# Moving modulation steps, DFT products and small loads in one step of a hybrid GLA and Fourier backbone

## The chip, the cores and the metric

The kernel runs on one core of a Trainium2 chip. The metric is the device time of one execution in microseconds (us), median of several runs. A profiled execution gives a trace of every instruction: TensorE (PE in the profile; PEld is its weight load), VectorE (DVE), ScalarE (ACT), GpSimd (POOL), and SP, which here only issues DMAs. All times below come from that profile or from the timed runs.

## The reference

One layer of a diffusion backbone for 128 context tokens and 256 latent tokens, 2048 channels, float32. Cut to what matters here:

```python
mod = jax.nn.silu(cond) @ lw['w_ada'] + lw['b_ada']
sh1, sc1, ga1, sh2, sc2, ga2 = [m[:, None, :] for m in jnp.split(mod, N_MOD, axis=-1)]
h = rmsnorm(x, lw['norm_pre_mix']) * (1.0 + sc1) + sh1
...
proj = h @ lw['w_in']                  # q, k, v, output gate g, two low-rank factors, Fourier channels fo
o = gla(q, k, v, decays)               # bidirectional gated linear attention, 4 heads
o = norm(o) * jax.nn.silu(g)
fg = fo.astype(jnp.float32).reshape(bsz, t, FOURIER_GROUPS, FOURIER_GROUP_DIM)
f = jnp.fft.fft2(fg, axes=(1, 3), norm='ortho').real
gates = jax.nn.sigmoid(h @ lw['w_gate'] + lw['b_gate'])
g_a, g_b = jnp.split(gates, 2, axis=-1)
merged = g_a * (o @ lw['w_br_gla']) + g_b * (f @ lw['w_br_four'])
return merged @ lw['w_out'], s_f, s_b
...
x = x + ga1 * rmsnorm(m, lw['norm_post_mix'])
h = rmsnorm(x, lw['norm_pre_ffn']) * (1.0 + sc2) + sh2
ff = (jax.nn.silu(h @ lw['w_ffn_gate']) * (h @ lw['w_ffn_up'])) @ lw['w_ffn_down']
x = x + ga2 * rmsnorm(ff, lw['norm_post_ffn'])
```

The six modulation vectors come from a product of one vector per token kind (context, latent) with a matrix of 2048 x 12288. The first two (sh1, sc1) are needed at once and are made on TensorE. Of the others, ga1 is needed by the output projection and sh2, sc2 by the FFN's input; these three, with the numbers 2, 3 and 4, are the "modulation steps" of this text.

## The kernel before

Activations lie transposed, channels on the 128 partitions and the 384 tokens along a row. A product in full float32 precision is made of three passes: every operand is split into a high part (`whi`, `A_hi`) and a low part (`wlo`, `A_lo`) of a reduced type, and high by high, high by low and low by high are summed.

**Weights.** A weight tile is 128 x 1024 (half a MB). `load` (L213) has SP fetch it into one of two `raw` buffers. `split` casts it to `whi` on ScalarE (L255) and subtracts on VectorE to `wlo` (L256); four pairs of buffers hold the results. `grab` takes the oldest ready pair, then loads one tile and splits one, so the split runs up to three tiles ahead of its use. For a tile of the Fourier projection (`fold`, L222 and L223) VectorE first adds and subtracts halves; for the two tiles of a DFT group it adds and subtracts the two raw tiles (L239, L240) and then splits both results (L316).

**Order.** PE, ScalarE, VectorE and GpSimd execute in the order in which the code is written. Side work is interleaved by generators: after every half unit (24 matmuls of 384 columns) `step` advances them. `paced(gen, rate)` advances one by `rate` calls to a step on average.

**Stages that the change touches**, in order of time:

- The head (up to 146 us): the normalised input is made and v is projected. `fold_h` adds and subtracts mirrored positions of h; `keep_h` (L417) stores the two halves of the folded h to DRAM, both by SP.
- 24 gate units (`gate_unit`, L673, L674), with GLA beside the first 22, one generator call to a half unit. In each head GpSimd clears `att` (L721) and `am` (L813), which VectorE then fills by masked copies. In the first 16 gate units SP also loads `wnr` (L902): the first column of 16 weight tiles, single words, needed by VectorE once (L933) behind gate unit 21.
- The DFT stage, gate units 24 to 31. Each is followed by two tiles of the Fourier input projection (`pfo`, L1038, L1039). After every second unit a group of 256 channels is complete; VectorE ends it in `fs` (L1043). The generator `dft` then makes products over channels (`px`, L995, L996 and L1001), copies them to `xc` and `nyq` (L997, L998, L1002), and makes products over positions in its next call (`pp`, L980, L981, L985).
- The output gates ("o", eight of them, `gcol`) and the Fourier projections ("b", sixteen, `four`), in the order of `mix_order` (L172): numbers of b behind each o are 0, 0, 1, 2, 2, 2, 1, 2. `nyq_weights` (L1058 to L1069) builds weights for the Nyquist row beside the first of them. `gate_of` fetches the sigmoid gate of a coming unit. Then come the GLA projections ("a") with the remaining b.
- The output projection (`wout`, 16 units), and behind it the FFN.

**Modulation steps.** `ada_rest` is a generator. For each of 3 vectors and each of 2 halves it makes 16 calls in which SP loads half a MB of `w_ada` (L621) and VectorE multiplies it by the condition of both token kinds and adds it to `adacc` (L624, L626); one empty call; one in which PE sums over partitions (`pr`, L634); and the next one begins by turning the result (`ptm`, L643) and adding biases. How many calls fall into each stage is set by `rate`:

```python
rate[0] = 1.0     # heads, 22 gate units;  0.5 in gate units 22 and 23;  1.0 in the DFT stage
rate[0] = 0.75    # output gates; 0.0 in Fourier and GLA projections
rate[0] = 0.7     # output projection
if i == KT - 4:   # behind its unit 12: whatever is left
    for _ in ada_gen:
        pass
```

Of the kernel before, what the change touches and what calls it, by code (L numbers as in the profile page):

```python
# [11 lines left out]
F32 = mybir.dt.float32  # L12
# [9 lines left out]
P = 128  # L22
# [85 lines left out]
def tile_step(ctx: ExitStack, tc: tile.TileContext, a, o):  # L108
# [60 lines left out]

    mix_order, n_b = [], 0  # L170
    for i in range(8):
        k = (0, 0, 1, 2, 2, 2, 1, 2)[i]  # L172
        mix_order += [("o", i)] + [("b", n_b + j) for j in range(k)]
        n_b += k
    for i in range(KT):
# [173 lines left out]
    with ExitStack() as s:  # L349
# [64 lines left out]
            ACT.copy(f[:, HL : HT : HC - 1], h[:, 0:HC : HC - 1])  # L414

        def keep_h(q):
            SP.dma_start(hf_d[:, 8 * q : 8 * q + 8, :], xnt[q])  # L417

        scr = actp.tile([P, 8, T], F32, tag="B_lo", name="scr")
        pv = [psm.tile([P, 512], F32, tag="mm", name="pv") for _ in range(3)]  # L420
# [257 lines left out]
    with ExitStack() as s:  # L678
# [20 lines left out]
        def chunks(x):  # L699
            return x.rearrange("p (t c i) -> p t c i", t=3, c=2)  # L700

        def gla():
            def split2(tags, src):
                out = [pg.tile([P, src.shape[1], src.shape[2]], F32R, tag=t, name="part") for t in tags]
# [8 lines left out]
            for h in range(NH):  # L713
# [5 lines left out]
                ACT.copy(krs, kr)  # L719
                att = pg.tile([P, 3, P], F32, tag="att", name="att")  # L720
                POOL.memset(att, 0.0)  # L721
                s0 = []
                for d in range(2):
                    s0.append(pg.tile([P, 1, DV], F32, tag=f"s0{d}", name="s0"))
# [86 lines left out]
                yield  # L811
                am = pg.tile([P, 3, CH], F32, tag="am", name="am")
                POOL.memset(am, 0.0)  # L813
                DVE.copy_predicated(am, mask[:, 1:2, :].to_broadcast([P, 3, CH]), ats[1])
                for c in range(2):
                    v = att[hf(c), :, c * CH : (c + 1) * CH]
# [80 lines left out]
        for i in QK[1:]:  # L897
            proj(psm, hT, keep(qk, i), sd)
        for i in range(GF):
            if i < 16:  # L900
                src = a["w_in"][16 + i // 2, i % 2].rearrange("p (k c) -> p k c", c=P)[:, :, 0]
                SP.dma_start(wnr[:, i // 2, 8 * (i % 2) : 8 * (i % 2) + 8], src)  # L902
            gate_unit(i, sd)
        for _ in gl:
            pass
# [3 lines left out]
    with ExitStack() as s:  # L909
# [67 lines left out]
        def dft():  # L977

            def even(dst, stat):
                PE.matmul(dst, stat(0, P), cd[:, D_TA : D_TA + HT], start=True, stop=False)  # L980
                PE.matmul(dst, stat(1, HC + 1), cd[0 : HC + 1, D_TB : D_TB + HT], start=False, stop=True)  # L981

            def odd(dst, stat):
                for k, m, c0, o0, o1 in ((0, HL - 2, D_SA, HC, HT), (1, HC - 2, D_SB, 0, HC)):
                    PE.matmul(dst[:, o0:o1], stat(k, m), cd[0:m, c0 : c0 + o1 - o0], start=True, stop=True)  # L985

            for g in range(4):
                while done[0] < g + 1:
                    yield
                fe, fd = fs[g]  # L990
                xc = [pf_.tile([P, 2, 2, P], F32, tag=f"xc{m}", name="xc") for m in range(2)]
                px = pss.tile([P, 2, 129], F32, tag="side", name="px")
                cb = D_CB + 129 * g
                for t, (p0, m) in enumerate(((0, P), (P, HC + 1))):
                    PE.matmul(px[0:m, t], fe[:, p0 : p0 + m], cd[:, D_CE : D_CE + 129], start=True, stop=False)  # L995
                    PE.matmul(px[0:m, t], bn[:, p0 : p0 + m], cd[:, cb : cb + 129], start=False, stop=True)  # L996
                    ACT.copy(xc[0][0:m, t], px[0:m, t, 0:P].unsqueeze(1).to_broadcast([m, 2, P]))  # L997
                    ACT.copy(nyq[0:m, t, g : g + 65 : 32], px[0:m, t, P : P + 1].to_broadcast([m, 3]))  # L998
                px = pss.tile([P, 2, P], F32, tag="side", name="px")
                for t, (p0, m) in enumerate(((0, HL - 2), (HL - 2, HC - 2))):  # L1000
                    PE.matmul(px[0:m, t], fd[:, p0 : p0 + m], cd[:, D_CS : D_CS + P], start=True, stop=True)  # L1001
                    ACT.copy(xc[1][0:m, t], px[0:m, t].unsqueeze(1).to_broadcast([m, 2, P]))  # L1002
                yield
                off = (P - 32 * g) % P
                rot = [x.rearrange("p t r c -> p t (r c)") for x in xc]
                for m, (x, part) in enumerate(((eT, even), (dT, odd))):
                    pp = pss.tile([P, HT], F32, tag="side", name="pp")
                    part(pp, lambda k, n: rot[m][0:n, k, off : off + P])
                    split_act(x[g][:, 0:HT], x[g][:, HT:], pp)
                yield  # L1010
            pn = pss.tile([P, HT], F32, tag="side", name="pn")
            even(pn, lambda k, n: nyq[0:n, k, :])
            ACT.copy(pnr, pn)
            DVE.tensor_sub(pnr[64:96], pn[64:96], pnr[64:96].bitcast(F32))
            yield
# [8 lines left out]

        sd = side()
        rate[0] = 1.0
        for i in range(FO0, 32):
            gate_unit(i, sd)
            g, kh = divmod(i - FO0, 2)
            if kh == 0:  # L1030
                pfo = [psm.tile([P, 2 * n], F32, tag="mm", name="pfo") for n in (HT, HO)]
                fs[g] = [pf_.tile([P, n], F32, tag=f"fs{j}", name="fs") for j, n in enumerate((HT, HO))]
            for j, n in enumerate((HT, HO)):
                w, p = grab(), pfo[j]
                for k in range(8):
                    x = xo[kh][:, k, :] if j else xe[:, 8 * kh + k].rearrange("p a c -> p (a c)")
                    c = slice(k * P, (k + 1) * P)
                    PE.matmul(p, w[0][:, c], x[:, 0 : 2 * n], start=kh == k == 0, stop=False)  # L1038
                    PE.matmul(p[:, 0:n], w[1][:, c], x[:, 0:n], start=False, stop=kh == 1 and k == 7)  # L1039
                if kh:  # L1040
                    f = fs[g][j]
                    ACT.copy(f, p[:, n : 2 * n])
                    DVE.tensor_add(f, f, p[:, 0:n])  # L1043
            if kh:
                done[0] = g + 1
        sx.close()
        fold_in.clear()
        pc = s.enter_context(tc.tile_pool(name="pc", bufs=1))
# [4 lines left out]
        def nyq_weights():  # L1053

            n = D // 2
            for h in range(2):
                wr = pc.tile([P, n], F32, tag="ws", name="wr")
                POOL.memset(wr, 0.0)  # L1058
                for g in range(4):
                    src = a["w_br_four"][8 * h : 8 * h + 8, 32 * g : 32 * g + 1, (2 * g + 1) * P : (2 * g + 2) * P]  # L1060
                    SP.dma_start(
                        wr[g : g + 65 : 32, :].rearrange("p (i c) -> p i c", c=P),
                        src.rearrange("i p c -> p i c").to_broadcast([3, 8, P]),
                    )
                    if g % 2:
                        yield
                w = wn[:, n * h : n * h + n]
                ACT.copy(w, wr)
                DVE.tensor_sub(w[32:64], wr[32:64], w[32:64].bitcast(F32))  # L1069
                yield  # L1070
# [67 lines left out]
        mT, late = None, []  # L1138
        for b, i in mix_order:
            if b == "o":  # L1140
                rate[0] = 0.75
                if i == 2:
                    gate_of()
                proj(psm, hT, lambda p: gcol(p, i), sd)
                if i == 2:
                    gate_of()
                rate[0] = 0.0
                continue
# [23 lines left out]
    with ExitStack() as s:  # L1172
# [42 lines left out]
            ACT.activation(sq2, mg32(i), AF.Square)  # L1215
            return sq0, pr, sq2

        rate[0] = 0.7
        spare_h = {-4: ((pe, "hid_hi", 1), (pe, "hid_lo", 1)), -2: ((pe, "S0", 1), (pe, "S1", 1))}
        spare_w = ((adap, "adaw", 2), (adap, "adaw", 2))  # L1220
        raw2 = None
# [926 lines left out]
```

## Time and profile before

| | us |
|---|---|
| median of 3 runs | 1976.55 (1975.61 to 1977.62) |
| the profiled execution | 1978.45 |
| its span, first to last instruction | 1976.7 |
| PE busy | 1912.3 (97%) |
| VectorE busy | 1673.7 (85%) |
| ScalarE busy | 1078.3 (55%) |
| GpSimd busy | 145.4 (7%) |
| mean granted TensorE clock | 0.990 |

Rows of the profile are read as follows. A group of instructions has its line, engine, operation, the tiles written and read, its shape and count, then busy time, mean length in ns, and the idle time of the engine just before, with what ended it. A list of waits has the waiting instruction, the one that released it, the total in us, how often, and the longest. A timeline has start, length and instruction, and in brackets the idle time before it. In a row by stage the window is followed by its length and by busy us and count of each engine, the granted clock, the share of DMA time and GB/s. Matmuls overlap, and their ends are modelled, so a PE that is always busy is not one at its peak.

### The profile page before, as it was taken

Reading aid. Unit: us, or ns where it says so; the run is one execution under the profiler, and the core shown is the slowest. Engines: PE = TensorE matmul, PEld = TensorE weight load, DVE = VectorE, ACT = ScalarE, POOL = GpSimd, SP = SyncE. Lnnn points to the kernel's source line nnn. Section 1 sums busy time; section 2 is a strip of 40 time slices with the busy share of each in tenths; the row PEclk is TensorE's granted clock in tenths of the full one; section 3 lists DMA queues with packets and bytes.
Section 4 is the critical chain, followed back from the end, with each engine's and each line's share of the span. In section 5 each row is a group of like instructions: output and inputs, shape, how many; then the busy total and the mean of one; then the engine's idle time right before and its main releaser. Section 6 shows DMA issues by size and latency. Waiting matters only on the chain.

```text
span 1976.7 us, 27848 instructions
## 1 busy us (share of the span) xinstructions
PE 1912.3 (97%) x10284; PEld 1682.4 (85%) x10284; DVE 1673.7 (85%) x2136; ACT 1078.3 (55%) x1566; POOL 145.4 (7%) x172
## 2 busy tenths in 40 slices
PE   8999999999998889997999999999999999999998
PEld 5778899998998789997998888888888888888886
DVE  5676898868758897796879999999999999988885
ACT  4234455453344555443746666666676766666555
POOL 0000000000000000000400021111111111202001
PEclk9999999999999999998999999999999999999999
DMA  9988666776655687565527796979697988969653
GB/s 390 370 300 222 231 221 229 249 259 226 206 191 171 207 276 268 180 206 176 205 93 241 200 253 167 277 155 279 146 267 171 245 199 221 235 155 241 168 196 125
DMA packets 263657, 435.65 MB, mean 220 GB/s; under 512 B 62044, under 2 KB 166684, under 8 KB 258912
## 3 DMA queue, kind: packets, MB, share of 16 engines
q1 hardware_dynamic: 216576, 393.23, 59.7%
q0 software_dynamic: 18432, 33.56, 11.2%
q10 hardware_dynamic: 28512, 7.08, 2.2%
q8 instruction: 80, 1.31, 0.3%
q14 instruction: 57, 0.47, 0.1%
HBM read 369.05 MB, written 57.67 MB: 216 GB/s over the span
## 4 chain that ended last, share of the span: by engine, by line
PE 82%; DVE 9%; DMA 4%; ACT 3%; issue 2%; SPq 0%; POOL 0%; DVEq 0%; ACTq 0%; POOLq 0%
PE pgu L1664 30%; PE pmm L289 23%; PE pdn L1664 10%; PE pds L1664 7%; DVE adacc L626 3%; PE pv L447 3%; DMA raw<-in_w_in 2%; DVE wlo L256 2%; PE pgm L430 1%; PE pfo L1038 1%; PE px L465 1%; PE pmm L1378 1%; ACT whi L255 1%; DMA adaw<-in_w_ada 1%; PE bk L1664 1%
## 5 line engine op out<-in xcount | busy, mean ns | idle before, releaser
L289 PE MATMUL pmm<-A_hi,wlo 128*128 128x384 f32 x1072 | 362.9, 339 | 5.4 <-DVE wlo L256 5.3
L289 PE MATMUL pmm<-A_hi,whi 128*128 128x384 f32 x1072 | 366.1, 341 | 0.0
L289 PE MATMUL pmm<-A_lo,whi 128*128 128x384 f32 x1072 | 362.5, 338 | 0.0
L1562 ACT CAST whi<-u 128x1024 fp32r<-128x1024 f32 x200 | 210.3, 1053 | 171.2 <-PE pds L1664 39.3
L1573 DVE TENSOR_TENSOR wlo<-u,whi 128x1024 fp32r<-128x1024 f32 x200 | 244.2, 1222 | 33.5 <-ACT whi L1562 29.0
L256 DVE TENSOR_TENSOR wlo<-raw,whi 128x1024 fp32r<-128x1024 f32 x163 | 198.7, 1222 | 69.9 <-ACT whi L255 69.3
L255 ACT CAST whi<-raw 128x1024 fp32r<-128x1024 f32 x165 | 172.7, 1050 | 152.3 <-DMA raw<-in_w_gate 52.4
L1664 PE MATMUL pgu<-whi,A_hi 128*128 128x512 f32 x640 | 249.9, 390 | 0.0
L1664 PE MATMUL pgu<-whi,A_lo 128*128 128x512 f32 x640 | 249.1, 389 | 0.0
L626 DVE SCALAR_TENSOR_TENSOR adacc<-adaw,cond,adacc 128x1024 f32<-128x1024 f32 x180 | 222.8, 1280 | 2.8 <-DMA adaw<-in_w_ada 2.6
L1562 ACT CAST whi<-raw 128x1024 fp32r<-128x1024 f32 x157 | 165.0, 1052 | 92.3 <-PE pgu L1664 25.8
L289 PEld LDWEIGHTS pmm<-A_hi,wlo 128*128 128x128 f32 x1072 | 204.1, 190 | 7.6 <-DVE wlo L256 7.3
L289 PEld LDWEIGHTS pmm<-A_hi,whi 128*128 128x128 f32 x1072 | 204.6, 191 | 4.3 <-issue 2.7
L289 PEld LDWEIGHTS pmm<-A_lo,whi 128*128 128x128 f32 x1072 | 204.3, 191 | 0.2
L1573 DVE TENSOR_TENSOR wlo<-raw,whi 128x1024 fp32r<-128x1024 f32 x157 | 191.6, 1221 | 12.4 <-ACT whi L1562 12.1
L1664 PE MATMUL pgu<-wlo,A_hi 128*128 128x512 f32 x640 | 185.8, 389 | 0.0
L1664 PEld LDWEIGHTS pgu<-whi,A_hi 128*128 128x128 f32 x640 | 120.1, 188 | 25.9 <-issue 0.8
L1664 PEld LDWEIGHTS pgu<-wlo,A_hi 128*128 128x128 f32 x640 | 120.1, 188 | 25.1
L1664 PEld LDWEIGHTS pgu<-whi,A_lo 128*128 128x128 f32 x640 | 120.1, 188 | 24.8
L1664 PE MATMUL pgu<-whi,S 128*128 128x512 f32 x400 | 116.6, 389 | 0.0
L1797 POOL DMA_DIRECT2D sums_d<-spare x64 | 58.4, 948 | 624.7 <-ACT spare L1793 607.8
L1664 PE MATMUL pdn<-whi,hid_hi 128*128 128x512 f32 x264 | 102.8, 389 | 0.0
(455 smaller groups left out, 3521.2 us busy)
## 6 DMA issues: line engine op xcount, KB each, us to landing
adaw<-in_w_ada SPq DMA_DIRECT2D x96, 512.0 KB, 3.7
raw<-in_w_d SPq DMA_DIRECT2D x70, 512.0 KB, 5.8
slab<-in_w_ada SPq DMA_DIRECT2D x32, 1024.0 KB, 9.0
raw<-in_w_gate SPq DMA_DIRECT2D x64, 512.0 KB, 4.5
raw<-in_w_g SPq DMA_DIRECT2D x48, 512.0 KB, 3.7
raw<-in_w_u SPq DMA_DIRECT2D x48, 512.0 KB, 5.1
u<-in_w_u SPq DMA_DIRECT2D x40, 512.0 KB, 5.6
u<-in_w_g SPq DMA_DIRECT2D x40, 512.0 KB, 9.3
```

What stands on the lines that cost most here:

```text
L255: ACT.copy(hi, raw)
L256: sub = lambda: eng.tensor_sub(lo, raw, hi.bitcast(F32))
L289: PE.matmul(dst, w[wi][:, k * n + n0 : k * n + n0 + P], x[xi][:, k0 + k, :], start=first and k == 0 and j == 0, stop=last and k == kts - 1 ...
L430: PE.matmul(pgv[q : q + 32, :], spad[:, k, :], slab[k // (KT // 2)][:, k % (KT // 2), :], start=k < 4, stop=k >= KT - 4,)
L447: PE.matmul(pv[2 * t + g], hT[x_][:, kb, t * P : (t + 1) * P], w_[:, g * 512 : (g + 1) * 512], start=kb == 0 and j == 0, stop=kb == KT - 1 ...
L465: PE.matmul(px, w_[:, u * P : (u + 1) * P], hT[x_][:, kb, :], start=j == 0, stop=j == 2)
L626: DVE.scalar_tensor_tensor(acc[:, c, :], w, cond[:, k, c : c + 1], acc[:, c, :], op0=ALU.mult, op1=ALU.add,)
L1038: PE.matmul(p, w[0][:, c], x[:, 0 : 2 * n], start=kh == k == 0, stop=False)
L1562: ACT.copy(hi, src)
L1573: DVE.tensor_sub(lo, src, hi.bitcast(F32))
L1664: PE.matmul(dst, stat[x_][m], mov(w[w_], m), start=first and w_ == m == x_ == 0, stop=last and w_ == m == 1, skip_group_check=any(more),)
L1797: POOL.dma_start(sums_d[k], u, accum_op=ALU.add)
```

## The change

- `mix_order`: the numbers of b behind each o become 0, 1, 1, 2, 1, 2, 1, 2. The two calls of `gate_of` go from output gate 2 to output gate 1.
- The rate at the output gates is 1.0 for the first two and 0.25 for the other six (0.75 before). In the DFT stage a second pacer on the same generator adds half a call for each of the two tiles of `pfo`. In the output projection the rate is 0.77 (0.7 before).
- In `dft` all products over channels of a group are issued ahead of the copies that read them; the second group of products has its own name, `py`.
- The second half of the folded h is stored by ScalarE's queue.
- The sixteen loads of single words go from SP to GpSimd's queue, as `column(n)`: two behind the memset of `att` in heads 1 to 3, two behind the memset of `am` in each head, two more in the last.
- The buffer `wr` in `nyq_weights` has its own place; before, it shared one with the folded weight tiles.

```diff
@@ mix_order
-        k = (0, 0, 1, 2, 2, 2, 1, 2)[i]
+        k = (0, 1, 1, 2, 1, 2, 1, 2)[i]
@@ keep_h
-            SP.dma_start(hf_d[:, 8 * q : 8 * q + 8, :], xnt[q])
+            (ACT if q else SP).dma_start(hf_d[:, 8 * q : 8 * q + 8, :], xnt[q])
@@ new function
+        def column(n):
+
+            src = a["w_in"][16 + n // 2, n % 2].rearrange("p (k c) -> p k c", c=P)[:, :, 0]
+            POOL.dma_start(wnr[:, n // 2, 8 * (n % 2) : 8 * (n % 2) + 8], src)
@@ gla
                 POOL.memset(att, 0.0)
+                if h:
+                    column(4 * h - 2)
+                    column(4 * h - 1)
...
                 POOL.memset(am, 0.0)
+                column(4 * h)
+                column(4 * h + 1)
+                if h == NH - 1:
+                    column(14)
+                    column(15)
@@ gate units
-            if i < 16:
-                src = a["w_in"][16 + i // 2, i % 2].rearrange("p (k c) -> p k c", c=P)[:, :, 0]
-                SP.dma_start(wnr[:, i // 2, 8 * (i % 2) : 8 * (i % 2) + 8], src)
@@ dft
                 for t, (p0, m) in enumerate(((0, P), (P, HC + 1))):
                     PE.matmul(px[0:m, t], fe[:, p0 : p0 + m], ..., start=True, stop=False)
                     PE.matmul(px[0:m, t], bn[:, p0 : p0 + m], ..., start=False, stop=True)
+                py = pss.tile([P, 2, P], F32, tag="side", name="py")
+                for t, (p0, m) in enumerate(((0, HL - 2), (HL - 2, HC - 2))):
+                    PE.matmul(py[0:m, t], fd[:, p0 : p0 + m], cd[:, D_CS : D_CS + P], start=True, stop=True)
+                for t, m in enumerate((P, HC + 1)):
                     ACT.copy(xc[0][0:m, t], px[0:m, t, 0:P].unsqueeze(1).to_broadcast([m, 2, P]))
                     ACT.copy(nyq[0:m, t, g : g + 65 : 32], px[0:m, t, P : P + 1].to_broadcast([m, 3]))
-                px = pss.tile([P, 2, P], F32, tag="side", name="px")
-                for t, (p0, m) in enumerate(((0, HL - 2), (HL - 2, HC - 2))):
-                    PE.matmul(px[0:m, t], fd[:, p0 : p0 + m], cd[:, D_CS : D_CS + P], start=True, stop=True)
-                    ACT.copy(xc[1][0:m, t], px[0:m, t].unsqueeze(1).to_broadcast([m, 2, P]))
+                for t, m in enumerate((HL - 2, HC - 2)):
+                    ACT.copy(xc[1][0:m, t], py[0:m, t].unsqueeze(1).to_broadcast([m, 2, P]))
@@ DFT stage
         rate[0] = 1.0
+        more = paced(ada_gen, [0.5])
...
                     DVE.tensor_add(f, f, p[:, 0:n])
-            if kh:
-                done[0] = g + 1
+                    if j:
+                        done[0] = g + 1
+                step(more)
@@ nyq_weights
-                wr = pc.tile([P, n], F32, tag="ws", name="wr")
+                wr = pc.tile([P, n], F32, tag="wr", name="wr")
@@ output gates
-                rate[0] = 0.75
-                if i == 2:
+                rate[0] = 1.0 if i < 2 else 0.25
+                if i == 1:
                     gate_of()
                 proj(psm, hT, lambda p: gcol(p, i), sd)
-                if i == 2:
+                if i == 1:
                     gate_of()
@@ output projection
-        rate[0] = 0.7
+        rate[0] = 0.77
```

## The prediction

> **What bounds the kernel now.** I read the page's busy shares and slices first, then the list of what TensorE (PE) waited for, then busy time by stage.
>
> ```profile
> PE   8999999999998889997999999999999999999998
> DVE  5676898868758897796879999999999999988885
> ```
>
> PE is busy all along, with dips at both ends, in the slices from 593 to 741 us and in the one from 890 (49.4 us each). So a gain can only come out of named gaps. The list of PE's waits names them (us in total, times, longest):
>
> ```profile
> PE pf L1113 <- DVE wlo L256: 10.3, 9, 1.5
> PE pr L634 <- DVE adacc L626: 10.1, 1, 10.1
> PE pmm L289 <- DVE wlo L256: 6.0, 6, 2.5
> PE px L995 <- ACT nyq L998: 5.8, 4, 4.2
> PE at L797 <- DVE ki L774: 5.1, 2, 4.6
> ...
> PE pf L1112 <- ACT whi L255: 2.2, 1, 2.2
> PE px L1001 <- ACT xc L1002: 2.2, 4, 0.6
> ```
>
> Stage by stage (window, length, then busy us and instructions of PE, its weight loads, VectorE, ScalarE, GpSimd; granted clock): the DFT stage, the first two output gates, the other gates with the Fourier projections, the output projection up to its unit 12 (with the last GLA projections), and what follows that unit.
>
> ```profile
> 452.90:578.20 125.30, 118.31 (x722) 114.39 (x719) 97.92 (x96) 48.54 (x77) 0.95 (x1) 0.97 0.64 204
> 578.20:609.00 30.80, 29.70 (x176) 28.89 (x175) 16.38 (x19) 11.51 (x21) 0.95 (x1) 1.00 0.46 153
> 609.00:709.00 100.00, 81.51 (x465) 75.52 (x464) 87.07 (x141) 52.77 (x78) 0.00 (x0) 0.98 0.67 220
> 779.00:895.00 116.00, 116.00 (x681) 115.07 (x679) 95.77 (x117) 51.83 (x83) 0.00 (x0) 1.00 0.61 198
> 895.00:912.00 17.00, 6.27 (x31) 4.25 (x30) 10.58 (x15) 2.01 (x5) 0.00 (x0) 0.61 0.40 129
> ```
>
> From 609 to 709 VectorE is busy 87% and PE stands still for 18.5 us, which are the first, third and sixth rows of the waits (10.3 + 6.0 + 2.2). The clock drops behind a gap, too; the same columns for three short windows:
>
> ```profile
> 489.10:495.90 6.80, 6.34 (x22) 5.71 (x21) 3.99 (x4) 2.11 (x5) 0.00 (x0) 0.50 0.73 233
> 615.30:618.70 3.40, 3.40 (x13) 3.40 (x12) 2.82 (x4) 2.08 (x3) 0.00 (x0) 0.51 0.92 322
> 707.50:710.90 3.40, 3.40 (x15) 3.40 (x15) 3.12 (x9) 2.83 (x7) 0.00 (x0) 0.50 0.62 202
> ```
>
> Half clock for 3.4 us costs 1.7 us of work.
>
> **The moved modulation steps.** One step is two products and sums on VectorE, half a MB loaded by SP, and every 17th and 18th call has no product. The first row is the page's cost; the others count such instructions by stage.
>
> ```profile
> L626 DVE SCALAR_TENSOR_TENSOR adacc<-adaw,cond,adacc 128x1024 f32<-128x1024 f32 x180 | 222.8, 1280 | 2.8 <-DMA adaw<-in_w_ada 2.6
> ```
> ```profile
> 452.90:578.20 125.30, 1.45 (x18) 0.70 (x18) 36.06 (x30) 0.37 (x1) 0.97 0.64 204
> 578.20:609.00 30.80, 0.00 (x0) 0.00 (x0) 4.96 (x4) 0.00 (x0) 1.00 0.46 153
> 609.00:709.00 100.00, 0.00 (x0) 0.00 (x0) 24.75 (x20) 0.00 (x0) 0.98 0.67 220
> 895.00:912.00 17.00, 2.85 (x18) 0.69 (x18) 7.35 (x6) 0.37 (x1) 0.61 0.40 129
> ```
>
> A step is 2 x 222.8/180 = 2.48 us of VectorE. The generator makes 109 calls. Before: 58 up to unit 23, 16 in the DFT stage (74), 16 x 0.75 = 12 at the output gates (86), 26 x 0.7 = 18 in the output projection (104), and 5 drained behind its unit 12. After: 58, 16 + 16 x 0.5 = 24 (82), 4 + 12 x 0.25 = 7 (89), 26 x 0.77 = 20 (109): nothing is left to drain. As products: 8 pairs (19.8 us of VectorE) more in the DFT stage, 6 pairs (14.9 us) fewer from 578 to 709, of which 8 fewer from 609 on and 2 more before it.
>
> *End of the drain.* VectorE's timeline there:
>
> ```profile
> 897.98 4.87 DVE L626 SCALAR_TENSOR_TENSOR adacc<-adaw,cond,adacc 128x1024 f32<-128x1024 f32 x4
> 904.04 2.48 DVE L626 SCALAR_TENSOR_TENSOR adacc<-adaw,cond,adacc 128x1024 f32<-128x1024 f32 x2 [1.19 <-DMA adaw<-in_w_ada]
> ```
>
> PE reduces `adacc` only behind these. After, the last pair is due at half-unit 23 (17/0.77) and the reduction at 25, 8 us later, so PE does not wait. The window 895 to 912 holds 31 matmuls: 18 of the reduction, which take 1.45 us at full clock (the 452.9 row), and 13 of the projection at 116/681 = 0.17 us, 3.7 us in all. Gain 17 - 3.7 = **13.3 us**. Its price: 16 pairs in 23 half-units (23 x 24 x 0.17 = 94 us) are 39 us; the rest of VectorE's work in 779 to 895 is 95.8 - 36 (15 pairs) = 60 in 116, or 48 in 94. 87 of 94 us: it still fits. If ScalarE's share does not let it, 4 us are lost (a rival below). I take 13.
>
> *Fourier projections.* What PE loses from 578 to 709 is 18.5 us, 2 x 1.7 of clock, and behind each of 16 gaps the modelled tail of a matmul (it lasts 0.34 and the next follows at 0.17), 2.7: 24.6 us. Without it the stage needs 130.8 - 24.6 - 1.1 (the fourth `px`) = 105 us of PE. VectorE: 16.4 + 87.1 - 14.9 = 88.6 busy, and waits that lie in its own chain (its groups in 609 to 709, idle time last):
>
> ```profile
> L256 DVE TENSOR_TENSOR wlo<-ws,whi 128x1024 fp32r<-128x1024 f32 x11 | 13.4, 1222 | 5.8 <-ACT whi L255 5.8
> ...
> L316 DVE TENSOR_TENSOR o_lo<-gs,o_hi 128x384 fp32r<-128x384 f32 x7 | 3.9, 558 | 4.1 <-ACT o_hi L315 4.1
> ```
>
> 98.5 us: under 105, but nearly level, so place decides. By pattern: two Fourier units and a gate now take VectorE about 16 us (window rows), PE 13.5; at rate 0.25 a pair fewer, 13.5. One Fourier unit and a gate: 9.7 against 11. The new order alternates them, so PE leads from the second unit on. The weak place is the first: unit b0 moves from behind the third gate to behind the second, where VectorE has 4 pairs, b0's fold and the copy of the Nyquist weights:
>
> ```profile
> 602.26 1.21 DVE L1069 TENSOR_TENSOR wn<-wr,wn 32x1024 fp32r<-32x1024 f32 x1 [2.73 <-ACT wn L1068]
> ```
>
> b0 itself reads only the first half of `wn`, but this second copy (behind a GpSimd memset and four DMAs) holds VectorE's queue, and queued behind it stand the split for o2's second half and b1's fold. I lay that queue out with these durations: o2's second half is about 3 us late, b1 about 4, each with one window of half clock: 10 us. Bounds: 0 (the wait falls into slack) to 16 (VectorE stays level to the end). Gain 24.6 - 10, I take **14 us** (8 to 24). The own buffer for `wr` only takes a dependency off; nothing.
>
> The Trainium skill, "TensorE: Matmul & The Clock Gate", Part 1, says that the clock falls to half after an idle window of about 3.4 us. This trace shows half clock at 615.3 behind a gap of 2.5 us at most; the measurement decides. By the page those clock windows would not hang on the gaps, and the stage would give 3 us less, 1945 in all.
>
> **DFT products ahead of copies.** Matmuls into `px` row tile 1 waited for ScalarE to read row tile 0 (fourth and last row of the waits, 8.0 us), and the 4.2 us gap of the first group brought 6.8 us of half clock, 3.4: 11.4 us. ScalarE's and PE's timeline:
>
> ```profile
> 485.91 1.05 ACT L315 CAST whi<-ws 128x1024 fp32r<-128x1024 f32 x1 [5.84 <-DVE ws L239]
> 487.17 1.04 ACT L315 CAST whi<-rp 128x1024 fp32r<-128x1024 f32 x1 [0.21 <-DVE rp L240]
> 488.12 0.36 ACT L997 COPY xc<-px 128x256 f32<-128x256 f32 x1
> ```
>
> The copies are not faster; they stand behind casts that wait for VectorE's `ws` and `rp`. After, PE goes on with half a gate unit (4.1 us), and needs the copies only at `pp`. Against it come the 8 pairs. VectorE: 97.9 + 19.8 = 117.7 us against 125.3 - 10 = 115: level again. Two calls without products (71, 72) fall to the third group, so groups 3 and 4 are free; in groups 1 and 2 the added pair before `fs` (2.48, less some 1.3 that VectorE idled there) makes `px` wait 1, and the one between `fs` and `ws` makes `pp` wait 2 and 1.4. 11.4 - 4.4 = **7 us**. Bounds: 11.4 if all is covered, and -8.4 if all 19.8 are exposed; nearer the first, since VectorE has 27 idle us here and 14 more up to 609. The moved steps bring their loads along, 8 x 0.5 MB: 204 GB/s (the stage row's last column) becomes some 240, and each waits on SP for a buffer that VectorE frees, with the next weight load queued behind; that follows VectorE's pace and adds no term of its own.
>
> **Folded h and single words.** One 1.5 MB store goes to ScalarE's queue: one issue (0.4 us, as SP's second row below) where ScalarE waits for the same fold anyway: nothing. The sixteen word loads leave SP's queue:
>
> ```profile
> L902 SPq DMA_DIRECT2D wnr<-in_w_in x16: 545/678/2943, 165.5 to 186.6; - x16
> ...
> 188.13 0.38 SPq L213 DMA_DIRECT2D raw<-in_w_in  x1
> ...
> 192.71 1.05 ACT L255 CAST whi<-raw 128x1024 fp32r<-128x1024 f32 x1 [7.56 <-DMA raw<-in_w_in]
> ```
>
> The load at 188 stood behind them, and the wait of `at` (5.1) is downstream of it. But SP then waits for free buffers instead, so I expect the load under 1 us sooner. Bounds 0 and 5.1 + 1.7; **1 us**. On GpSimd each costs between the mean of its present DMAs and eight times that (1,024 words against 128 rows):
>
> ```profile
> L1797 POOL DMA_DIRECT2D sums_d<-spare x64 | 58.4, 948 | 624.7 <-ACT spare L1793 607.8 <-DMA u<-in_w_g 10.4 <-ACT whi L1562 6.5
> ...
> L797 PE MATMUL at<-qi,ki x96: 222/222/356, 197.1 to 381.3; 128*64 128x64 f32 x96
> ```
>
> 0.95 to 7.6 us, four to a head, and a head lasts about 60 us ((381.3 - 197.1)/3): 4 x 7.6 = 30, covered, with the memsets of `att` and `am` queued behind.
>
> **Sum.** 7 + 14 + 13 + 1 = 35 us. The profiled execution took 1978.45 (span 1976.7 and 1.75 around it): 1943.5. It is 1.9 above the median 1976.55, so **1941.5 us**.
>
> **Rivals.** (a) *VectorE becomes the bound of the DFT stage*: for it, 117.7 against 115; against, the idle time up to 609. Then that term is -8.4, and its delay leaves 10 of the Fourier term: 16 us, 1961. (b) *No new wait at b0 and b1, none at `pp`*: 11 + 22 + 13 + 1 = 47, 1929.5; for it, that PE holds up to three weights ready. (c) *VectorE is full in the output projection*: 4 us less, 1945.5; for it, 87 of 94 us. (d) *The waits only move*, since VectorE's total is unchanged: what is left is the end of the half clock at 489, 3 us, 1973.5; against, 40 idle us of VectorE before 609. (e) *Slower: the word loads hold GpSimd.* Place: `att` and `am` memsets behind them, with VectorE's masked copies, then weights, waiting. From 15 us a load (60/4) each head slips by 4t - 60; over four heads this eats the 35 us at t = 17. At 25 us it is 160 us, 2101. Against: even the slowest present rate by count is 7.6.
>
> The Trainium skill, "SBUF — State Buffer", SBUF: two separate sides, says that GpSimd's descriptors starve while VectorE runs a two-port operation; it gives 3,100 ns for a DMA of 620. By that ratio, 5 x 7.6 = 38 us, (e) would hold. No run here shows it: GpSimd's DMAs at 0.95 us lie beside VectorE's two-input operations, and these are also what fills the heads.
>
> **Chances.** Forecast 0.45, (a) 0.20, (b) 0.17, (c) 0.10, (d) 0.04, (e) 0.04. Range 1927 to 1962: from under (b) to over (a). About 0.2% (4 us) is what a measurement tells from no change: faster 0.92, same 0.04, slower 0.04.
>
> **What would show it.** Right: no wait of `px` on `nyq`, no `pr` wait near 900, under 12 us of `pf`/`pmm` waits from 578 to 709, the first at o2 or b1; SP without `wnr`. Wrong: waits of PE on `wlo` in the DFT stage (a), on `pmm` before 895 (c), VectorE waiting for GpSimd's memsets (e).

## The result and the profile after

The changed kernel takes **1946.05 us**, median of 4 runs (1945.23 to 1947.25), against 1976.2 (4 runs, 1975.61 to 1977.62) of the kernel before: a ratio of 0.9847, 95% interval 0.983 to 0.9864, or 30.2 us faster. The forecast was 1941.5, and the range (1927 to 1962) holds the time. The profiled execution took 1945.23 us, its span is 1943.3.

The page's busy shares and the slices of PE and VectorE, of the kernel after (a slice is 48.6 us):

```profile
PE 1901.4 (98%) x10284; PEld 1676.0 (86%) x10284; DVE 1671.0 (86%) x2136; ACT 1078.5 (55%) x1568; POOL 159.4 (8%) x188
...
PE   8998999999998999999999999999999999999997
...
DVE  5677888878997797987789999999999999988985
```

The dips that stood between 593 and 741 us and at 890 are gone but for one 8 at 583 to 632. VectorE's count of instructions is what it was; its work sits earlier.

The list of PE's waits from 459 to 760, kernel after (us in total, times, longest):

```profile
PE pf L1127 <- DVE wlo L256: 5.0, 6, 1.5
PE pf L1126 <- ACT whi L255: 2.0, 1, 2.0
PE py L1009 <- DVE fs L1056: 1.6, 1, 1.6
PE pmm L289 <- DVE wlo L256: 1.5, 1, 1.5
PE pfo L1052 <- DVE wlo L316: 0.8, 1, 0.8
PE pp L990 <- ACT xc L1011: 0.7, 2, 0.3
PE pfo L1051 <- ACT whi L315: 0.5, 1, 0.5
PE pf L1129 <- DVE edT L1026: 0.5, 1, 0.5
```

`px` waits for no `nyq` any more, and no `pr` waits for `adacc`. The windows used in the prediction no longer cut the same work, so from here on stages are bounded by named instructions of PE: the first `pfo` (DFT), the first `pt` (transposes of the first output gate), the last `pf` (end of the Fourier projections), the first `pst` (behind the output projection), the first `bk` (last block). The stage rows of before and then of after (window, length, busy us and instructions of PE, its weight loads, VectorE, ScalarE, GpSimd; granted clock, DMA share, GB/s):

```profile
461.38:589.63 128.25, 120.16 (x731) 115.68 (x731) 94.47 (x94) 48.87 (x81) 0.95 (x1) 0.97 0.67 213
589.63:764.54 174.91, 156.42 (x909) 150.20 (x908) 151.26 (x254) 90.68 (x141) 0.95 (x1) 0.98 0.68 223
764.54:935.29 170.75, 160.02 (x927) 157.08 (x927) 131.40 (x165) 73.44 (x118) 0.00 (x0) 0.96 0.60 197
...
1945.26:1976.70 31.44, 22.49 (x121) 18.28 (x119) 17.96 (x53) 16.90 (x47) 6.41 (x5) 0.95 0.35 101
```
```profile
459.42:580.34 120.92, 117.24 (x732) 112.66 (x731) 112.89 (x111) 45.63 (x80) 0.96 (x1) 1.00 0.80 249
580.34:742.82 162.48, 153.35 (x909) 149.78 (x907) 135.67 (x240) 93.94 (x143) 0.96 (x1) 0.98 0.70 227
742.82:899.79 156.97, 156.97 (x926) 155.24 (x926) 126.55 (x164) 73.68 (x118) 0.00 (x0) 1.00 0.63 209
...
1910.13:1943.30 33.17, 22.49 (x121) 18.28 (x119) 17.95 (x53) 16.90 (x47) 6.40 (x5) 0.94 0.33 95
```

The DFT stage is 7.3 us shorter although VectorE does 18.4 us more in it; the Fourier stage 12.4 shorter; in the output projection PE is busy for all of 156.97 us, 13.8 shorter. What lies ahead of them ("heads" in the table below) is 2.0 shorter. Up to the last block the gain is 35.1 us. Then the last row: the same matmuls, the same busy times on every engine, and **1.7 us longer**. Left of the span's gain: 33.4.

### The profile page after: what moved, and what is told of

The parts are those of the page before. It is cut to its first block, busy times and chain, and to the rows that moved or that the text cites. A ratio compares the mean times of both kernels' runs of the same rounds, so it can differ in the third digit from the quotient of the medians.

```text
span 1943.3 us, 27865 instructions
## 1 busy us (share of the span) xinstructions
PE 1901.4 (98%) x10284; PEld 1676.0 (86%) x10284; DVE 1671.0 (86%) x2136; ACT 1078.5 (55%) x1568; POOL 159.4 (8%) x188
## 4 chain that ended last, share of the span: by engine, by line
PE 82%; DVE 8%; DMA 4%; ACT 3%; issue 2%; SPq 0%; POOL 0%; ACTq 0%; DVEq 0%; POOLq 0%
PE pgu L1678 31%; PE pmm L289 23%; PE pdn L1678 10%; PE pds L1678 7%; PE pv L447 3%; DVE adacc L626 3%; DMA raw<-in_w_in 2%; PE pgm L430 1%; DVE wlo L256 1%; DMA slab<-in_w_ada 1%; PE px L465 1%; PE pmm L1392 1%; PE bk L1678 1%; DMA adaw<-in_w_ada 1%; ACT whi L255 1%
## 5 line engine op out<-in xcount | busy, mean ns | idle before, releaser
L1587 DVE TENSOR_TENSOR wlo<-u,whi 128x1024 fp32r<-128x1024 f32 x200 | 243.9, 1221 | 33.4 <-ACT whi L1576 31.3
```

What stands on the lines that cost most here:

```text
L1587: DVE.tensor_sub(lo, src, hi.bitcast(F32))
```

## The experiments

The table gives, for each kernel that ran, how much longer (+) or shorter (-) each stage is than in the kernel before, worked out from the starts of the instructions named above in its one profiled execution. Kernels whose code for a stage is the same differ in it: by up to 2.9 us in the heads (eight kernels, -2.6 to +0.3), by up to 3.4 in the DFT stage (seven kernels, -8.7 to -5.3), by 0.9 in the Fourier stage (three kernels). Smaller differences are not read. Kernels for which no interval is given ran once. Each experiment ran beside runs of the kernel before, with medians of 1978.5 to 1980.0 us there, and its ratio is to those; so medians of the experiments and the 1946.05 above are not compared directly.

| kernel | heads | DFT | Fourier | output proj. | last block | span |
|---|---|---|---|---|---|---|
| after | -2.0 | -7.3 | -12.4 | -13.8 | +1.7 | 1943.3 |
| order alone | 0.0 | -11.9 | +0.9 | +0.3 | 0.0 | 1966.1 |
| rate 0.89 alone | +2.2 | +0.4 | -0.3 | -13.8 | 0.0 | 1965.2 |
| after, twice the added steps | -1.5 | +10.0 | -9.8 | -15.2 | +2.1 | 1962.3 |
| after, Nyquist slower | -2.3 | -8.7 | -16.3 | -13.8 | +1.7 | 1938.1 |
| after, folded h on SP | -3.7 | -6.9 | -12.3 | -13.8 | +2.1 | 1942.3 |
| after, words on SP | -1.5 | -8.6 | -11.5 | -13.8 | 0.0 | 1941.3 |
| after, old order of units | -2.6 | -8.5 | -14.1 | -13.8 | +2.4 | 1940.5 |
| Nyquist slower, other rates (0, 0.89) | -0.1 | -8.1 | -20.9 | -13.8 | +1.7 | 1935.9 |
| the same (more 0.25, 0.1, 1.0) | -0.8 | -10.3 | -18.0 | -13.4 | +2.6 | 1937.1 |
| the same (more 0.375, 0.1, 0.95) | +0.3 | -9.6 | -17.2 | -13.8 | +1.9 | 1938.3 |
| (0, 0.89), old order of units | -1.3 | -5.3 | -22.8 | -13.8 | +2.6 | 1936.5 |
| words on GpSimd alone | -4.5 | +1.0 | +0.2 | +0.1 | +1.7 | 1975.1 |

**Products ahead of copies, alone.** The kernel before with the new order in each DFT group:

```diff
+ py = pss.tile([P, 2, P], F32, tag="side", name="py")
+ for t, (p0, m) in enumerate(((0, HL - 2), (HL - 2, HC - 2))):
+     PE.matmul(py[0:m, t], fd[:, p0 : p0 + m], ...)
  ... copies of px into xc[0] and nyq, then
- px = pss.tile(...); PE.matmul(px[0:m, t], fd ...); ACT.copy(xc[1] ... px)
+ ACT.copy(xc[1][0:m, t], py[0:m, t]...)
```

> The kernel before with one edit: the products over channels of a DFT group ahead of the copies. Theory: PE's waits at px (8.0 us) and the half clock behind the first (3.4 us) go, and nothing comes in their place, since VectorE has 27 idle us in this stage: the first transpose of the output gates comes 10 us sooner (9 to 11.4). Rival: the copies are as late as before, so PE waits for them one half unit later, at pp: 3 to 5 us sooner.

Measured: the DFT stage is 11.9 us shorter, and the list of PE's waits from 459 to 600 holds one row:

```profile
PE pfo L1041 <- DVE wlo L316: 0.2, 1, 0.2
```

So the new order is worth all of the 11.4 us that the prediction counted (a little more than the 9 to 11.4 expected here), with no wait for a copy at `pp`. The whole change gains 7.3 there, so in its profiled execution the added modulation steps cost 4.6; with the scatter of that stage (gains of 5.3 to 8.7 from the same code) it is some 3 to 7. The run took 1968.1 us.

**The drain, alone.** The kernel before with a higher rate in the output projection, so that nothing is left to drain, and no step moved elsewhere:

```diff
- rate[0] = 0.7
+ rate[0] = 0.89
```

> The kernel before with one edit: rate 0.89 in place of 0.7 in the output projection, so that the drain behind unit 12 is empty without moving a step to another stage. Theory: the 10 us wait at pr goes, but 18 pairs now lie in 94 us, beside 48 us of other VectorE work and ScalarE's waits: VectorE is full, and PE waits for wlo inside the stage: 8 us gained of 13 (5 to 10). Rival: VectorE has room, and moving steps out of this stage was not needed: 13 us.

Measured: the same 13.8 us as in the whole change, in a run of 1967.68. My theory of a VectorE with no room fell. Stage row, then VectorE's groups from 779 to 895 (busy us, mean ns, idle time before and what ended it), kernel with rate 0.89:

```profile
766.82:923.79 156.97, 156.97 (x926) 155.24 (x926) 130.12 (x166) 73.31 (x118) 0.00 (x0) 1.00 0.65 215
...
L256 DVE TENSOR_TENSOR wlo<-raw,whi 128x1024 fp32r<-128x1024 f32 x28 | 34.1, 1220 | 10.4 <-ACT whi L255 10.4
...
L1202 DVE TENSOR_TENSOR qs<-qs,sq 128x384 f32<-128x384 f32 x11 | 6.1, 552 | 2.1 <-ACT sq L1191 2.1
```

The same two groups in the kernel before:

```profile
L256 DVE TENSOR_TENSOR wlo<-raw,whi 128x1024 fp32r<-128x1024 f32 x28 | 34.1, 1222 | 12.3 <-ACT whi L255 12.1
...
L1202 DVE TENSOR_TENSOR qs<-qs,sq 128x384 f32<-128x384 f32 x11 | 6.1, 557 | 5.9 <-ACT sq L1191 5.8
```

Part of the idle time that this expectation had taken for VectorE's load gives way when VectorE comes later: what it waited for is then there already (5.9 to 2.1, 12.3 to 10.4). That part was slack, not load. For this stage no step had to be moved elsewhere.

**Twice the added steps in the DFT stage.**

```diff
- more = paced(ada_gen, [0.5])
+ more = paced(ada_gen, [1.0])
...
- rate[0] = 0.77
+ rate[0] = 0.47
```

> The changed kernel with twice as many added steps in the DFT stage (16 calls in place of 8) and rate 0.47 in the output projection, so that the total is the same. Theory: VectorE has 137 us of work in a stage of which PE needs 115; PE waits there and at the first output gates: 15 us slower than the changed kernel (10 to 20). Rival: the stage still had idle VectorE time, and the steps hide: 0 to 5 us slower.

Measured: the DFT stage is 17.3 us longer than in the changed kernel, within what the theory expected. PE's waits from 459 to 760:

```profile
PE pfo L1051 <- ACT whi L315: 7.0, 4, 3.3
PE pf L1127 <- DVE wlo L256: 6.2, 5, 1.5
PE pf L1126 <- ACT whi L255: 3.3, 2, 2.0
PE pfo L1052 <- DVE wlo L316: 3.3, 4, 0.8
...
```

Against the list of after, `pfo` now waits 10.3 us instead of 1.3. VectorE does become the bound of this stage, as the prediction's rival (a) has it, only not at the eight pairs of the change: those cost 4.6, the next lot 17. This run took 1964.83.

**One piece of the Nyquist weights per call instead of two,** in the changed kernel:

```diff
- for _ in range(2):
-     next(nw, None)
+ next(nw, None)
```

> The changed kernel with one edit: the builder of the Nyquist weights advances once per half unit in place of twice, so that the copy of the second half (which only Fourier units from 8 on read) comes behind the third output gate. Theory: the 2.7 us in which VectorE waits for that copy are what makes o2's second half and unit b1 late; these waits (1.5 + 2.0 + 1.5 us) and 6.8 us of half clock behind them go: 6 us faster than the changed kernel (3 to 8.5). Rival: VectorE is level with PE in this stage, and the same time is lost at the next Fourier units: 0 to 2 us.

Here is the weak place that the prediction named, in the kernel after: VectorE's timeline (start, length, instruction, idle time before), and the granted clock behind it:

```profile
595.91 1.22 DVE L1083 TENSOR_TENSOR wn<-wr,wn 32x1024 fp32r<-32x1024 f32 x1 [2.70 <-ACT wn L1082]
597.15 2.48 DVE L626 SCALAR_TENSOR_TENSOR adacc<-adaw,cond,adacc 128x1024 f32<-128x1024 f32 x2
599.55 1.22 DVE L256 TENSOR_TENSOR wlo<-raw,whi 128x1024 fp32r<-128x1024 f32 x1
...
608.00 1.22 DVE L256 TENSOR_TENSOR wlo<-ws,whi 128x1024 fp32r<-128x1024 f32 x1
```
```profile
600.83 0.45 PE L289 MATMUL pmm<-A_hi,wlo 128*128 128x384 f32 x1 [1.49 <-DVE wlo L256]
607.28 0.45 PE L1126 MATMUL pf<-edT,whi 128*128 128x388 f32 x1 [2.01 <-ACT whi L255]
609.27 0.53 PE L1127 MATMUL pf<-edT,wlo 128*128 128x194 f32 x1 [1.54 <-DVE wlo L256]
```
```profile
608.10:614.90 6.80, 5.63 (x20) 5.63 (x21) 4.09 (x4) 3.54 (x5) 0.00 (x0) 0.50 0.67 215
```

With the second copy coming later, the waits of `pmm` and of `pf` on `whi` are gone from the list, and the whole Fourier stage runs at full clock:

```profile
PE pf L1127 <- DVE wlo L256: 7.6, 7, 1.5
PE pfo L1052 <- DVE wlo L316: 0.8, 1, 0.8
PE py L1009 <- DVE fs L1056: 0.7, 1, 0.7
```
```profile
578.71:737.30 158.59, 150.86 (x908) 147.10 (x907) 134.41 (x238) 92.33 (x141) 0.95 (x1) 1.00 0.71 230
```

That stage is 3.9 us shorter. PE's idle time in it falls from 9.1 to 7.7 us: waits of 2.0, 1.5 and 0.5 go, and the waits of `pf` on `wlo` grow from 5.0 to 7.6. Its busy time falls by 2.5, which is the clock: 5.63 us busy at half clock hold 2.8 of work. The median is 1942.14 (4 runs), ratio 0.9815 [0.9798, 0.9831]: better than the changed kernel by about 6 us by the ratios, though the intervals just touch. The theory held for the copy's waits and the clock, and the rival for part of the gain: 2.6 us are waited at later Fourier units instead.

**Old order of the units,** with the new rates (and the gate fold back at the third gate):

```diff
- k = (0, 1, 1, 2, 1, 2, 1, 2)[i]
+ k = (0, 0, 1, 2, 2, 2, 1, 2)[i]
...
- if i == 1:
+ if i == 2:
```

> The changed kernel with the old order of Fourier units behind the output gates (0, 0, 1, 2, 2, 2, 1, 2) and the old place of the first gate, but the new rates. Theory: the pairs of Fourier units that follow each other take VectorE as long as PE, so the waits on wlo there come back in part, while those of the first unit go: 4 us slower than the changed kernel (2 to 8). Rival: the rates alone made the gain of this stage: within 2 us.

Measured: 1943.1 us, and the Fourier stage 1.6 us shorter than in the changed kernel. PE's waits there (waits of the DFT stage left out):

```profile
PE pf L1127 <- DVE wlo L256: 6.6, 8, 1.5
PE pmm L289 <- DVE wlo L256: 2.5, 1, 2.5
```

My theory fell. Alternating the units does not put PE ahead; it brings the first Fourier unit up to the copy of the Nyquist weights, and `pf` waits for `wlo` either way. With the order of units out, and the stage unmoved by the DFT order and by rate 0.89 alone (+0.9 and -0.3), what is left of the change here is the modulation steps taken out of it and the own buffer for `wr`. That buffer did not run by itself; VectorE's wait at the copy of `wn` is 2.7 us with it (2.70) and without it (2.73).

**Other rates.** If that is so, taking the rest of the steps out of this stage, into the output projection that has room, should gain again. On top of the slower Nyquist pieces:

```diff
- rate[0] = 1.0 if i < 2 else 0.25
+ rate[0] = 1.0 if i < 2 else 0.0
...
- rate[0] = 0.77
+ rate[0] = 0.89
```

> e4_nyq with no modulation step at the output gates from the third on (rate 0 in place of 0.25), and 0.89 in the output projection, which the run e2_drain had shown to fit. Theory: the waits left at the Fourier units (7.6 us in e4_nyq) come from VectorE being level with PE; two pairs (5 us) fewer there, and none of them missed in the output projection: 4 us faster than e4_nyq (2 to 7). Rival: these waits are ScalarE's chain of fold, cast and subtraction, not VectorE's load: within 1 us.

Measured: 1937.47 us (4 runs), ratio 0.9793 [0.9776, 0.9809]; the intervals of this and of the kernel with slower Nyquist pieces overlap, but the Fourier stage is another 4.6 us shorter, and the waits of `pf` are halved:

```profile
PE pf L1127 <- DVE wlo L256: 3.8, 5, 1.5
```

So half of those waits hang on VectorE's load; what holds up the other half stays open.

Two more divisions, with fewer steps in the DFT stage and an output projection at rates 1.0 and 0.95:

```diff
- more = paced(ada_gen, [0.5])
+ more = paced(ada_gen, [0.25])        # the second: [0.375]
...
+ rate[0] = 1.0 if i < 2 else 0.1
...
+ rate[0] = 1.0                        # the second: 0.95
```

> e8_rates with 4 added calls in the DFT stage in place of 8, 5 at the output gates in place of 4, and one to every half unit (rate 1.0) in the output projection, which then holds 22 pairs (54.6 us) beside some 54 us of other VectorE work in 106 us. Theory: the DFT stage gives back 2 to 3 us of the 4 that the added steps cost it there, and the output projection is now just full, so PE waits for wlo there up to 3 us: 1 us faster than e8_rates (-2 to +3). Rival: the output projection still has room: 2.5 us faster; or it falls behind by all that it is over and the reduction waits again: 3 us slower or more.

> Between e8_rates and e9_rates2: 6 added calls in the DFT stage, 5 at the output gates, rate 0.95 in the output projection. Theory: 1 us faster than e8_rates (0 to 2), with no wait of PE in the output projection. Rival: as for e9_rates2.

Measured: 1938.32 us, ratio 0.98 [0.9785, 0.9814], and 1938.02, ratio 0.9794 [0.9777, 0.9811]: neither can be told from the one before, and neither theory's gain is seen. The Fourier stage gives back 3.0 and 3.7 us; what the DFT stage gains (2.1 and 1.5) is within its scatter. The output projection at rate 1.0 still leaves PE no gap to speak of, though in the stretch with the most steps (second row) VectorE is full:

```profile
735.53:892.86 157.33, 157.19 (x926) 155.14 (x926) 137.17 (x174) 73.45 (x118) 0.00 (x0) 1.00 0.68 225
797.00:867.00 70.00, 69.86 (x413) 68.71 (x412) 69.72 (x78) 28.77 (x48) 0.00 (x0) 1.00 0.67 225
```

And the division (0, 0.89) with the old order of units:

> e8_rates with the old order of Fourier units behind the output gates. e7_mix had shown the old order 1.6 us faster in this stage, with the first unit's waits in play; here these are gone. Theory: with VectorE relieved the order decides nothing: within 1.5 us of e8_rates. Rival: units that follow each other are late by VectorE's chain, as the kernel before had it: 3 us slower.

Measured: 1935.65 us (1932.12 to 1939.12), ratio 0.9785 [0.9766, 0.9804]: the fastest median, not told from its neighbours by these intervals, and some 12 us below the changed kernel by the ratios. The Fourier stage is 1.9 us shorter with the old order, a little more than the 1.5 expected and a second time in that direction. (The DFT stage came out 2.8 longer with code that is the same.)

**Folded h and single words, each put back on SP.** Two kernels, in each of which one of the two goes back to SP's queue:

```diff
- (ACT if q else SP).dma_start(hf_d[:, 8 * q : 8 * q + 8, :], xnt[q])
+ SP.dma_start(hf_d[:, 8 * q : 8 * q + 8, :], xnt[q])
```

> The changed kernel with the second store of the folded h back on SP. Theory: ScalarE waited for the same fold anyway, so no stage moves: the first product of the Fourier stage (bnp) at 436 as in the changed kernel (within 0.7 us). Rival: SP's release is the gain of these edits: back to 438 to 440 as before.

```diff
- column(4 * h) ...                    # every call in the heads
  for i in range(GF):
+     if i < 16:
+         src = a["w_in"][16 + i // 2, i % 2]...
+         SP.dma_start(wnr[:, i // 2, ...], src)
```

> The changed kernel with the sixteen loads of single words back on SP. Theory: these are the whole gain of 2 us in the heads, since SP's weight loads queued behind them: bnp back to 438 to 440. Rival: the gain lies elsewhere, or is noise of the DMAs at the start: bnp stays at 436.

Measured: 1944.21 and 1943.33 us. In the heads neither takes the 2 us away (-3.7 and -1.5 us against before): `bnp` starts at 434.2 with the folded h on SP and at 436.4 with the words on SP (435.9 in the changed kernel, 437.9 before). Neither is what its theory expected, and one execution can't decide: with equal code up to there `bnp` starts anywhere from 435.3 to 438.2. But the last block shows what neither expectation has: with the words on SP it takes 31.4 us again, as in the kernel before:

```profile
1909.86:1941.30 31.44, 22.49 (x121) 18.29 (x119) 17.95 (x53) 16.91 (x47) 6.41 (x5) 0.96 0.35 101
```

Sorted by that, the kernels fall into two sets without exception: 31.4 us where the words go by SP (before, order alone, rate alone, words on SP), 33.2 and more where they go by GpSimd (the other nine above). The surplus lies behind the last byte of the stores, where no engine has an instruction. The rows of that stretch, before, words on SP, and after:

```profile
1975.10:1976.70 1.60, 0.00 (x0) 0.00 (x0) 0.00 (x0) 0.00 (x0) 0.00 (x0) 0.50 0.00 0
```
```profile
1939.70:1941.30 1.60, 0.00 (x0) 0.00 (x0) 0.00 (x0) 0.00 (x0) 0.00 (x0) 0.50 0.00 0
```
```profile
1940.00:1943.30 3.30, 0.00 (x0) 0.00 (x0) 0.00 (x0) 0.00 (x0) 0.00 (x0) 0.50 0.00 0
```

(Where the table has +2.1 to +2.6, the last transposes run at half clock besides: sixteen of them took 1.97 us in the kernel before and in the changed one, 3.19 with twice the added steps.)

**The words on GpSimd, alone,** in the kernel before, to try that sorting by one edit:

```diff
+ def column(n): ... POOL.dma_start(wnr[:, n // 2, ...], src)
+ column(...)                          # in the heads, as in the changed kernel
- if i < 16: ... SP.dma_start(wnr[:, i // 2, ...], src)
```

> The kernel before with only the sixteen word loads moved from SP's queue to GpSimd's; all else as before. Two questions. At the end: in the traces so far the four kernels whose words go by SP end 1.6 us behind the last byte of their stores, and the nine whose words go by GpSimd end 3.1 to 3.3 us behind it, with no instruction in either stretch. Theory: the loads on GpSimd's queue are what lengthens the end, so this kernel ends about 3.3 us behind its last byte, and from the first matmul of the last block to the end 33.2 us pass (31.4 before). Rival: the length of the end hangs on something else in the changed kernel or on chance; then 31.4. In the heads: theory, the 2 us that the changed kernel gained come from SP being free of the words, and the first gate fold's matmul (before 437.9) starts near 436; rival, it is scatter between executions, and it starts within 1.5 us of 438 on either side. Nothing else should differ: in all 0 to 2 us slower by the theory of the end with no gain in the heads, and no change if both theories hold.

The last block, and the stretch behind the last byte:

```profile
1941.99:1975.13 33.14, 22.48 (x121) 18.28 (x119) 17.96 (x53) 16.91 (x47) 6.41 (x5) 0.93 0.33 95
```
```profile
1972.00:1975.10 3.10, 0.00 (x0) 0.00 (x0) 0.00 (x0) 0.00 (x0) 0.00 (x0) 0.50 0.00 0
```

The theory of the end held: sixteen small loads on GpSimd's queue at 149 to 334 us make the program end 1.7 us later, at 1975. By what, these records don't show. The run also says something on the heads. Its median is 1977.39 (11 runs) against 1978.53 (15 runs), ratio 0.9997 [0.9988, 1.0006], that is 0.6 us faster by the ratio, give or take 1.8. If nothing else differs, the end costs 1.7 and so the heads gain 2.3 on the mean, 0.5 to 4.1; its one profiled execution shows 4.5. That points to some 2 us in the heads for an SP free of the words, nearly all of which the end gives back; it is not shown, as the words put back on SP left 1.5 of the 2.0 there, and that kernel's span was 2.0 us shorter than the changed one's. What the folded h brings stays open: it is less than the scatter.

## Why the prediction was right, and where not

**End of the drain, 13 us: right, 13.8.** Its price was right too: "87 of 94 us" adds up busy time alone, and it fits, with no wait of PE in the stage. Rival (c) is out. The stage held more than that: 18 pairs at rate 0.89, and at rate 1.0 as many as fill VectorE (69.72 of 70 us), with PE idle for 0.14 us.

**DFT stage, 7 us: right, 7.3.** It came about as laid out: 11.9 for the order, 4.6 for the added steps (predicted 11.4 and 4.4). That 4.4 and 4.6 agree is in part luck, since the stage scatters by 3.4 and the places were off: not `px` 1 and `pp` 2 and 1.4, but `py` on `fs` 1.6, `pfo` 0.8 and 0.5, `pp` 0.7. The 0.8 is a wait on `wlo`, the sign that the prediction had named for rival (a). Rival (a) was nearer than the list of waits shows, as the run with twice the added steps shows: eight more pairs, and the stage is 10 us slower than before.

**Fourier stage, 14 us: right in size, 12.4, with half of its reasons.** The weak place was where the prediction put it and of the kind it named: VectorE's queue held 2.70 us by the copy of `wn`, then o2's second half late (1.49) and b1 late (2.01 and 1.54), with half clock for 6.8 us, in which PE was busy for 5.63 and so lost 2.8. Together 7.8 of the 10 us set aside. The step that failed is "the new order alternates them, so PE leads from the second unit on": later `pf` still wait 3.5 us (5.0 less the 1.54 at b1), and the old order does no worse. What remains for the gain is the rates: fewer modulation steps in the stage, which the prediction had counted as 14.9 us of VectorE. That its sum came near without the lead of PE is in part luck. The waits of `pf` and `pmm` come to 9.0 us (5.0, 2.0, 1.5 and 0.5), under the 12 that the forecast allowed. The first of them is not quite where it was expected: 0.5 us at b0, for `edT` (593.27), and then o2's.

**Heads, 1 us: mis-sized by the end.** The heads gained 2.0 in the profiled execution and 2.3 in the runs of the words alone, within the bounds 0 and 6.8 but no more than the scatter. The wait of `at`, which was to be downstream of the loads, is 3.5 us instead of 5.1. But "on GpSimd each costs between 0.95 and 7.6 us" looked only at the place of the loads. They cost 0.88 each there (tile `wnr` in the kernel after: duration min, median, max in ns, first and last start):

```profile
L705 POOL DMA_DIRECT2D wnr<-in_w_in x16: 880/880/1077, 151.5 to 336.7; - x16
```

and 1.7 us at the end of the program, which no term held. Rival (e) is out: 0.88 is far from the 17 us from which it decides. The Trainium skill, "SBUF — State Buffer", SBUF: two separate sides, has such a DMA take 3,100 ns instead of 620 when GpSimd's descriptors starve; the trace shows no such factor: 0.88 us for GpSimd, and from issue to landing 5.6 us at the median against 3.5 on SP's queue before.

**The sum.** 35 us were forecast, 35.1 were there at the first matmul of the last block, and the end took 1.7 back: own time 1945.23 where 1943.5 was laid out. That is 1.7 of the 4.5 us between 1941.5 and the median 1946.05. The other 2.8 are the step from one execution to the median: I took off 2.0 because the profiled execution of before lay that far above its median, while that of after lies 0.8 below its own.

Of the other rivals, (b) assumed that nothing waits at b0 and b1, which is not what the changed kernel does; slower Nyquist pieces and other rates come most of the way there (1936 to 1938). (d) is out: the waits went.

The half clock behind short gaps held only in part. In the changed kernel 0.50 begins at 608.1, behind the gap of 2.01 us (up to 607.28) and inside the one of 1.54. Behind o2's 1.49 the clock stayed 1.00 (600.8 to 607.5), so the one window set aside there did not come, and lone gaps of 2.97 and 2.22 us in the heads (before 162.50 and 169.43) brought none either. The Trainium skill, "TensorE: Matmul & The Clock Gate", Part 1, asks for an idle window of about 3.4 us; here, as at 615 in the kernel before, none was that long. The 1945 that the prediction worked out from this rule lies nearer to 1946.05 than the forecast does, but by luck: with slower Nyquist pieces the half clock of this stage goes where the longer gaps go, and the difference lies in the end and in the step to the median. Which gaps bring half clock these runs don't settle.

## What to carry to other kernels

Count an engine's load by its busy time and treat the idle time inside its own chain as slack, unless it still stands there when the engine comes later; a trial of one rate settled it here for the price of one run. Look for a single instruction that waits at the head of an in-order queue (here a copy behind four small loads) before reordering the units around it. When a load moves to another queue, compare the end of the program too, behind the last byte.

## What was not expected of the hardware

Sixteen loads of 1,024 single words each took GpSimd 0.88 us apiece, a little less than its other DMAs (0.95 and 1.15), and left far fewer packets on record. The page's count of DMA packets, before and after:

```profile
DMA packets 263657, 435.65 MB, mean 220 GB/s; under 512 B 62044, under 2 KB 166684, under 8 KB 258912
```
```profile
DMA packets 247530, 435.65 MB, mean 224 GB/s; under 512 B 45917, under 2 KB 150557, under 8 KB 242785
```

16,127 packets fewer for the same bytes, and 16,128 (to 247529) where the words alone were moved. There the packets of queue q1 fall by 16,640 and those of q0 ("software_dynamic") rise by 512, so the 16,384 words are on record as some 512 packets. The price is the longer end behind the last store, 3.0 to 3.3 us instead of 1.6, which every kernel with these loads on GpSimd's queue showed and none without them.
